# Ten SBUF buffers of split weights: starts at ten different offsets in place of multiples of 2048

## The chip, the cores and the metric

The kernel runs on one core of one Trainium2 chip. The core has TensorE (PE in the profile; its weight loads are listed apart as PEld), VectorE (DVE), ScalarE (ACT), GpSimd (POOL) and SyncE (SP), which here issues all transfers. On-chip memory is SBUF, 128 partitions of which each engine reads and writes the same byte range of all partitions at once, and PSUM, into which matmuls accumulate. The metric is device time in microseconds of one execution; the median of several runs counts.

## What is computed

Two layers on 1024 tokens of width 1024, all in fp32. Layer 0 is attention over a sliding window with sinks, layer 1 a gated linear recurrence (HGRN2); each is followed by an MLP with a squared ReLU, and a norm ends it.

```python
for layer in range(DEPTH):
    h = rmsnorm(x, mix_norm[layer])
    if layer % N_MIXERS == 0:
        y = sliding_window_attention(h, positions, attn_w_qkv[j], attn_b_qkv[j], attn_sinks[j], attn_w_o[j])
    else:
        y = hgrn2_recurrence(h, lbs[layer], hgrn_w_in[j], hgrn_g_norm[j], hgrn_w_o[j])
    x = x + y.astype(x.dtype)
    h = rmsnorm(x, mlp_norm[layer])
    x = x + sqrelu_mlp(h, mlp_w_up[layer], mlp_w_down[layer]).astype(x.dtype)
return rmsnorm(x, final_norm)
```

Nearly all the work is matrix products with weights: QKV and output projections, the four input projections of the recurrence, and 1024 x 4096 up and 4096 x 1024 down in each MLP.

## The kernel before

**Split products.** Weights arrive in fp32. To multiply them in the format fp32r, `weight_split` (line 412) makes two tiles of each 128 x 512 tile: `wh`, the weight rounded to fp32r (a cast on ScalarE or VectorE, whichever the planner finds free), and `wl`, the rest that rounding left (a subtraction on VectorE). Activations are split the same way into pairs of `a` or `t` tiles. `mm3` (line 394) then makes three matmuls of each product: high by high, high by low, low by high. So of three loads of weights two come from a `wh` tile and one from a `wl` tile. In all products but one the split weights are the stationary operand, which LDWEIGHTS puts into TensorE in blocks of 128 columns (512 bytes of each partition), and 512 or 256 columns of activations stream past them. In `qkv` (line 1069) it is the other way: the activations are loaded and 512 columns of `wh` or `wl` stream. In the profile `p<-a,wh` is a matmul that streams an `a` tile, with weights from a `wh` tile, into a PSUM tile of kind p.

The large products follow Strassen's scheme in Winograd's form, which saves products and pays with sums of weight blocks (`m` tiles, on VectorE) and of activations. A weight that is split therefore lies in a `wr` tile (raw, as the transfer brought it), in an `m` tile (a sum of weights) or, in the MLP's down product, in an `a` tile.

**Order.** The program is first recorded as a list of operations with costs in ns (`Schedule.add`). `Schedule.order` (line 185) then plays it through: each engine takes the ready operation of best rank, and each tile gets a slot of its kind, the one that comes free first. `BUFS` (line 41) says how many slots a kind has. The order that this gives is what each engine's queue gets. The costs are constants and functions of the number of columns; no address enters.

**Places in SBUF.** `Buf.handle` (line 111) makes the tile of a slot when it is first used, under a tag such as `wh_3`. All tiles of one tag share one place, as large as the largest of them. Tags are laid one behind the other, each rounded up to 32 bytes. `lay_out` (line 473) runs before all operations are issued and fixes the first places: some constants, then 60 `a`, 18 `t`, 5 `wr`, 5 `wh` and 5 `wl` tiles of 2048 bytes a partition. In the allocation of this kernel the first `a` tile begins at 18432 = 9 x 2048, so all of these lie on multiples of 2048. What comes behind is laid in the order of first use: other constants, the seven `m` buffers and the small `sm` ones. An `m` buffer has 2080 bytes, since attention makes an `m` tile of 128 x 4 x 130 floats (`attend_block`, line 1166, one row group j of 520 bytes for each of four heads). The `m` buffers begin at 209920, 212000 and so on, which is 1024, 1056, 1088, 1120, 1152, 1184 and 1216 past a multiple of 2048.

In attention, ScalarE takes the exponential of each row group of an `m` tile in place (`ACTIVATE m<-m,sm` of 128 x 129), and TensorE transposes each row group (`q<-c,m`: the constant identity streams, the row group is loaded).

Of the kernel before, what the change touches and what calls it, by code (L numbers as in the profile page):

```python
# [2 lines left out]

# [7 lines left out]
F32 = mybir.dt.float32  # L11
# [6 lines left out]
P = 128  # L18
# [4 lines left out]
TH = T // NH  # L23
# [17 lines left out]
BUFS = {"a": 60, "t": 18, "m": 7, "sm": 8, "wr": 5, "wh": 5, "wl": 5, "p": 4, "q": 4}  # L41
CH = 64
LEVELS = 6
HOMES = "aaaaaaaaaaaa"
K_SPANS = ((-1, 3), (2, 6), (5, 8))


class View:
# [34 lines left out]
class Buf:  # L83
# [27 lines left out]
    def handle(self):  # L111
        if self.tile is None:
            tag = f"{self.tag}_{self.slot}"
            self.tile = self.pool.tile(self.shape, self.dtype, tag=tag, name=self.name, bufs=1)
        return self.tile


# [24 lines left out]
class Schedule:  # L142
# [132 lines left out]
    def issue(self, lay_out):  # L275
        ops = self.order()
        lay_out()
        for op in ops:
            op.ways[op.engine][0]()


class Net:
# [190 lines left out]
    def lay_out(self):  # L473

        for v in (self.par, self.ones, self.ident, self.prev_mask, self.mean, self.eps, self.neg, *self.square[:1]):
            v.buf.handle()
        for tag in ("a", "t", "wr", "wh", "wl"):
            for k in range(BUFS[tag]):
                self.pool.tile([P, TH], F32, tag=f"{tag}_{k}", name=f"{tag}_first{k}", bufs=1)

    def spread(self, y, n=TH, r=None):

        r = (r or self.psum("q"))[:, :n]
        for j in range(n // P):
            self.mm(r[:, j * P : j * P + P], y[:, j : j + 1].to_broadcast([P, P]), self.ident, True, True, P, 4)
        return r
# [549 lines left out]
    def k_tiles(self, i):  # L1036
        if self.ks[i] is None:
# [3 lines left out]
            for g, z in enumerate(self.kl[i]):  # L1041
                _, o = self.rows(g)
                self.memset(z[o].bitcast(F32).only("o"), 0.0, "Pool", late)
            if K_SPANS[i][0] < 0:
                for z in self.ks[i] + self.kl[i]:
# [51 lines left out]
    def keys_values(self, n, ps, r):  # L1097
# [14 lines left out]
        for gp in range(2):  # L1112
            self.transpose(pk[:, gp], k[:, gp * P : gp * P + P])
        for i, (first, end) in enumerate(K_SPANS):
            if not first <= n < end:
# [50 lines left out]
    def attend_block(self, g, n, stacks):  # L1166
        i = (n >= 3) + (n >= 6)
        c = slice((n - 1 - K_SPANS[i][0]) * P, (n + 1 - K_SPANS[i][0]) * P)
        tok = slice((n % BPH) * P, (n % BPH) * P + P)
# [485 lines left out]
```

## Time and profile before

| what | value |
|---|---|
| median of 3 runs | 2102.72 us (2101.64 to 2105.72) |
| the profiled execution: its time | 2103.77 us |
| the profiled execution: first to last instruction | 2102.0 us |
| instructions | 35648, of which 12220 matmuls with as many weight loads |
| DMA | 407 MB in the span, 58.5% of the 16 engines' time |

A row of the groups gives the engine and operation, the tiles written and read, the shape and how often; behind the bar the busy time in us and the mean ns of one, then the idle time of the engine ahead of it and what ended that. A row of a tile's view gives the least, median and greatest ns of one. Matmul records overlap: the time that a matmul costs TensorE is the distance between two starts, not its duration. In the chain of work that ended last and in the timeline the first number is the start in us, the second how long the piece lasted, and `x192` says that 192 instructions are merged in it.

### The profile page before, as it was taken

Reading aid. Unit: us, or ns where it says so; the run is one execution under the profiler, and the core shown is the slowest. Engines: PE = TensorE matmul, PEld = TensorE weight load, DVE = VectorE, ACT = ScalarE, POOL = GpSimd, SP = SyncE. Lnnn points to the kernel's source line nnn. Section 1 sums busy time; section 2 is a strip of 40 time slices with the busy share of each in tenths; the row PEclk is TensorE's granted clock in tenths of the full one; section 3 lists DMA queues with packets and bytes.
Section 4 is the critical chain, followed back from the end, with each engine's and each line's share of the span. In section 5 each row is a group of like instructions: output and inputs, shape, how many; then the busy total and the mean of one; then the engine's idle time right before and its main releaser. Section 6 shows DMA issues by size and latency. Waiting matters only on the chain.

```text
span 2102.0 us, 35648 instructions
## 1 busy us (share of the span) xinstructions
PE 2068.4 (98%) x12220; PEld 1738.6 (83%) x12220; DVE 1898.4 (90%) x3922; ACT 1120.0 (53%) x2284; POOL 61.0 (3%) x121
## 2 busy tenths in 40 slices
PE   9999999999999999999999999999999999999998
PEld 7778777888888887888888888888788888888887
DVE  8889899999999989999889888888999999998995
ACT  5567777656565323556444444443755656432453
POOL 4030000000000000000000000000000000000000
PEclk9999999999999999999999999999999999999999
DMA  6212277867778967732322232576787777896742
GB/s 214 79 51 81 86 239 245 297 224 248 231 240 289 313 220 245 236 136 76 101 98 99 96 101 97 202 234 221 270 267 229 244 228 250 284 321 211 238 133 80
DMA packets 225845, 407.43 MB, mean 194 GB/s; under 512 B 25344, under 2 KB 30464, under 8 KB 225664
## 3 DMA queue, kind: packets, MB, share of 16 engines
q1 hardware_dynamic: 225664, 405.16, 58.5%
q8 instruction: 96, 1.57, 0.3%
q14 instruction: 85, 0.70, 0.1%
HBM read 321.17 MB, written 83.89 MB: 193 GB/s over the span
## 4 chain that ended last, share of the span: by engine, by line
PE 38%; DVE 11%; DMA 4%; issue 3%; ACT 1%; POOL 0%; SPq 0%; POOLq 0%; DVEq 0%; ACTq 0%
PE p L336 22%; PE q L336 16%; DVE t L336 4%; DVE a L336 3%; DMA wr<-in_down 2%; DVE wl L336 2%; DVE m L336 2%; ACT t L336 1%; DMA t<-d 1%; DMA wr<-in_up 1%; DMA d<-t 0%; DVE wh L336 0%; DMA wr<-in_win 0%; DMA a<-d 0%; ACT wh L336 0%
## 5 line engine op out<-in xcount | busy, mean ns | idle before, releaser
L336 PE MATMUL p<-a,wh 128*128 128x512 f32 (+1 forms) x2880 | 809.9, 365 | 3.2 <-DVE a L336 2.4
L336 PE MATMUL q<-a,wh 128*128 128x512 f32 x2112 | 654.6, 391 | 7.4 <-ACT t L336 6.1
L336 PEld LDWEIGHTS p<-a,wh 128*128 128x128 f32 x2880 | 514.6, 189 | 89.1 <-DVE a L336 4.0
L336 PE MATMUL p<-a,wl 128*128 128x512 f32 (+1 forms) x1440 | 521.0, 362 | 0.4 <-DVE wl L336 0.4
L336 PEld LDWEIGHTS q<-a,wh 128*128 128x128 f32 x2112 | 389.1, 188 | 85.3 <-ACT t L336 8.4
L336 PE MATMUL q<-a,wl 128*128 128x512 f32 x1056 | 411.1, 390 | 1.7 <-DVE wl L336 1.7
L336 PEld LDWEIGHTS p<-a,wl 128*128 128x128 f32 x1440 | 271.6, 189 | 40.9 <-DVE wl L336 1.3
L336 DVE TENSOR_TENSOR wl<-wr,wh 128x512 fp32r<-128x512 f32 x352 | 240.8, 685 | 6.7 <-ACT wh L336 1.3
L336 DVE TENSOR_TENSOR wl<-m,wh 128x512 fp32r<-128x512 f32 x338 | 230.1, 686 | 10.6 <-ACT wh L336 1.4
L336 PEld LDWEIGHTS q<-a,wl 128*128 128x128 f32 x1056 | 198.3, 188 | 45.6 <-DVE wl L336 3.7
L336 ACT ACTIVATE t<-t 128x512 f32<-128x512 f32 x268 | 168.8, 632 | 122.3 <-DVE t L336 114.9
L336 ACT CAST wh<-wr 128x512 fp32r<-128x512 f32 x249 | 154.0, 619 | 142.8 <-PE p L336 94.7
L336 DVE TENSOR_TENSOR t<-t,t 128x512 f32<-128x512 f32 (+3 forms) x337 | 197.4, 599 | 17.0 <-DMA t<-d 9.9
L336 ACT CAST a<-t 128x512 fp32r<-128x512 f32 (+1 forms) x216 | 130.1, 611 | 148.5 <-PE q L336 78.7
L336 DVE TENSOR_TENSOR a<-t,a 128x512 fp32r<-128x512 f32 (+2 forms) x314 | 205.9, 677 | 2.2 <-ACT a L336 1.7
L336 ACT CAST wh<-m 128x512 fp32r<-128x512 f32 x231 | 143.1, 620 | 113.8 <-PE p L336 47.4
L336 ACT COPY t<-q 128x512 f32<-128x512 f32 (+2 forms) x201 | 112.2, 559 | 104.1 <-PE q L336 87.3
L336 DVE TENSOR_TENSOR m<-wr,wr 128x512 f32<-128x512 f32 (+1 forms) x188 | 120.9, 645 | 17.6 <-DMA wr<-in_down 13.0
L336 PE MATMUL p<-wh,a 128*128 128x512 f32 x384 | 124.9, 396 | 0.7 <-ACT a L336 0.7
L336 DVE TENSOR_TENSOR t<-t,p 128x256 f32<-128x256 f32 x294 | 118.0, 414 | 0.3
L336 PEld LDWEIGHTS q<-t,t 128*64 128x64 f32 (+1 forms) x2160 | 95.4, 144 | 13.6 <-issue 7.6
L336 PE MATMUL q<-t,t 128*64 128x32 f32 (+2 forms) x2160 | 105.3, 229 | 0.0
(129 smaller groups left out, 2392.7 us busy)
## 6 DMA issues: line engine op xcount, KB each, us to landing
t<-d SPq DMA_DIRECT2D x548, 256.0 KB, 4.1
d<-t SPq DMA_DIRECT2D x244, 256.0 KB, 2.7
wr<-in_down SPq DMA_DIRECT2D x224, 256.0 KB, 4.2
wr<-in_up SPq DMA_DIRECT2D x178, 256.0 KB, 3.9
wr<-in_win SPq DMA_DIRECT2D x68, 256.0 KB, 2.9
a<-d SPq DMA_DIRECT2D x60, 256.0 KB, 4.7
wr<-in_wqkv SPq DMA_DIRECT2D x48, 256.0 KB, 2.9
d<-a SPq DMA_DIRECT2D x48, 256.0 KB, 3.9
```

The source lines that it names most:

```text
L336: fn(*[place(a) for a in args], **{k: place(v) for k, v in kw.items()})
```

## The change

The ten buffers `wh_0` to `wh_4` and `wl_0` to `wl_4` are laid alternately, and each gets some unused floats in front, so that its data begin at the listed number of bytes past a multiple of 2048:

| buffer | wh_0 | wl_0 | wh_1 | wl_1 | wh_2 | wl_2 | wh_3 | wl_3 | wh_4 | wl_4 |
|---|---|---|---|---|---|---|---|---|---|---|
| before | 0 | 0 | 0 | 0 | 0 | 0 | 0 | 0 | 0 | 0 |
| after | 4 | 40 | 80 | 96 | 128 | 192 | 256 | 384 | 512 | 768 |
| floats in front | 1 | 2 | 4 | 0 | 8 | 16 | 16 | 32 | 32 | 64 |

`handle` makes the larger tile and hands out a view of it without the floats in front; all else that works on the tile is unchanged. Everything laid behind the ten moves by 768 bytes.

```diff
+W_STARTS = (4, 40, 80, 96, 128, 192, 256, 384, 512, 768)
+SKIP = {}
+_end = 0
+for _k, _start in enumerate(W_STARTS):
+    SKIP[f"{('wh', 'wl')[_k % 2]}_{_k // 2}"] = (_start - _end) // 4
+    _end = -(-_start // 32) * 32
...
             tag = f"{self.tag}_{self.slot}"
-            self.tile = self.pool.tile(self.shape, self.dtype, tag=tag, name=self.name, bufs=1)
+            skip = SKIP.get(tag, 0)
+            if skip:
+                n = math.prod(self.shape[1:])
+                whole = self.pool.tile([self.shape[0], skip + n], self.dtype, tag=tag, name=self.name, bufs=1)
+                self.tile = whole[:, skip:]
+                if len(self.shape) == 3:
+                    self.tile = self.tile.rearrange("p (a b) -> p a b", a=self.shape[1])
+            else:
+                self.tile = self.pool.tile(self.shape, self.dtype, tag=tag, name=self.name, bufs=1)
...
-        for tag in ("a", "t", "wr", "wh", "wl"):
+        for tag in ("a", "t", "wr"):
             for k in range(BUFS[tag]):
                 self.pool.tile([P, TH], F32, tag=f"{tag}_{k}", name=f"{tag}_first{k}", bufs=1)
+        for k in range(BUFS["wh"]):
+            for tag in ("wh", "wl"):
+                name = f"{tag}_{k}"
+                self.pool.tile([P, TH + SKIP[name]], F32, tag=name, name=f"{tag}_first{k}", bufs=1)
```

More of the change, by code (lines that the diff above doesn't have):

```diff
@@ L1 @@
 import heapq
+import math
 from contextlib import ExitStack
```

## The prediction

> **What bounds the kernel now.** I read the page first: the busy shares, the clock the chip granted, then the chain of work that ended last.
>
> ```profile
> span 2102.0 us, 35648 instructions
> PE 2068.4 (98%) x12220; PEld 1738.6 (83%) x12220; DVE 1898.4 (90%) x3922; ACT 1120.0 (53%) x2284; POOL 61.0 (3%) x121
> ...
> PEclk9999999999999999999999999999999999999999
> ...
> PE 38%; DVE 11%; DMA 4%; issue 3%; ACT 1%; POOL 0%; SPq 0%; POOLq 0%; DVEq 0%; ACTq 0%
> PE p L336 22%; PE q L336 16%; DVE t L336 4%; DVE a L336 3%; DMA wr<-in_down 2%; DVE wl L336 2%; DVE m L336 2%; ACT t L336 1%; DMA t<-d 1%; DMA wr<-in_up 1%; DMA d<-t 0%; DVE wh L336 0%; DMA wr<-in_win 0%; DMA a<-d 0%; ACT wh L336 0%
> ```
>
> The matmul stream fills the span and the clock is never held back. The chain names PE for the largest share; the making of split weights (DVE wl, DVE wh, ACT wh) has 2%, 0% and 0% of it. So the first question is what one matmul takes and whether it depends on where its weights lie. The trace's matmul durations overlap, so I take the distance between starts. The chain in order of time has three unbroken stretches at the end, and the timeline of PE has a stretch of 256-column matmuls:
>
> ```profile
> 1965.90 32.71 PE p L336 x143
> 1998.61 43.52 PE q L336 x192
> 2042.13 21.76 PE p L336 x96
> ```
> ```profile
> 400.08 0.40 PE L336 MATMUL p<-t,wh 128*128 128x256 f32 x2
> 400.32 0.28 PE L336 MATMUL p<-t,wl 128*128 128x256 f32 x1
> ...
> 401.40 0.28 PE L336 MATMUL p<-t,wl 128*128 128x256 f32 x1
> 401.52 0.63 PE L336 MATMUL q<-a,wh 128*128 128x512 f32 x2
> ```
>
> 43.52 us over 192 is 226.7 ns for 512 columns; 21.76 over 96 is the same. From 400.08 to 401.52 twelve matmuls start (four rounds of three), 120 ns each for 256 columns. The difference, 106.7 ns for 256 columns, is 0.417 ns a column, and 13.3 ns of each matmul are left over, alike in both sizes. Where that rest comes from the trace doesn't say; the weight load that runs beside each matmul is the nearest candidate. The loads themselves, from the views of the tiles wh and wl (least, median, greatest ns):
>
> ```profile
> L336 PEld LDWEIGHTS p<-a,wh x2880: 186/188/193, 186.3 to 2063.1; 128*128 128x128 f32 x192
> L336 PEld LDWEIGHTS q<-a,wh x2112: 186/188/192, 322.4 to 2041.3; 128*128 128x128 f32 x192
> L336 PEld LDWEIGHTS p<-t,wh x392: 187/192/192, 387.9 to 1776.5; 128*128 128x128 f32 x196
> L336 PE MATMUL p<-wh,a x384: 387/389/504, 5.7 to 186.3; 128*128 128x512 f32 x192
> ```
> ```profile
> L336 PEld LDWEIGHTS p<-a,wl x1440: 186/188/192, 186.7 to 2063.3; 128*128 128x128 f32 x180
> L336 PEld LDWEIGHTS q<-a,wl x1056: 186/188/192, 322.9 to 2041.5; 128*128 128x128 f32 x176
> L336 PEld LDWEIGHTS p<-t,wl x196: 187/192/192, 388.2 to 1776.6; 128*128 128x128 f32 x196
> L336 PE MATMUL p<-wl,a x192: 387/389/477, 6.0 to 186.0; 128*128 128x512 f32 x192
> ```
>
> These six kinds of load come to 2880 + 2112 + 392 + 1440 + 1056 + 196 = 8076; another 384 + 192 = 576 matmuls stream the split weights instead. Two groups of the lines by form give the 256-column part:
>
> ```profile
> L336 PE MATMUL p<-a,wh 128*128 128x256 f32 x784 | 145.5, 283 | 0.3 <-DVE t L336 0.3
> ...
> L336 PE MATMUL p<-a,wl 128*128 128x256 f32 x392 | 110.5, 283 | 0.0
> ```
>
> With the 392 + 196 on t that is 1764 of the 8076; 6312 have 512 columns.
>
> **The change part by part.** It takes no instruction away and adds none: each split buffer becomes a view that begins up to 256 bytes (64 floats) into a slightly larger tile. The planner orders work by costs, none of which knows an address, so order, waits and transfers stay. No DMA writes or reads wh or wl. What can change is the time of an instruction that touches one of the ten, and of those that touch what is laid behind them (m, sm, later constants), which moves by 768 bytes.
>
> *The buffers behind.* In the allocation of the kernel before, the seven m buffers begin at 1024, 1056, 1088 and so on to 1216 past a multiple of 2048. 768 is a multiple of 256, so each keeps its place against every smaller boundary. I cost this at nothing.
>
> *VectorE and ScalarE.* Those m buffers are the trace's own test of uneven starts: three of seven lie 32 bytes past a multiple of 64, while wr lies on multiples of 2048. The same operation with the one and with the other:
>
> ```profile
> L336 DVE TENSOR_TENSOR wl<-wr,wh 128x512 fp32r<-128x512 f32 x352 | 240.8, 685 | 6.7 <-ACT wh L336 1.3 <-PE q L336 0.5 <-DVE wh L336 0.5
> L336 DVE TENSOR_TENSOR wl<-m,wh 128x512 fp32r<-128x512 f32 x338 | 230.1, 686 | 10.6 <-ACT wh L336 1.4
> ...
> L336 ACT CAST wh<-wr 128x512 fp32r<-128x512 f32 x249 | 154.0, 619 | 142.8 <-PE p L336 94.7 <-PE q L336 27.2 <-DMA wr<-in_down 5.5
> ...
> L336 ACT CAST wh<-m 128x512 fp32r<-128x512 f32 x231 | 143.1, 620 | 113.8 <-PE p L336 47.4 <-PE q L336 41.4 <-DVE m L336 24.8
> ...
> L336 DVE CAST wh<-m 128x512 fp32r<-128x512 f32 x107 | 45.6, 426 | 33.6 <-PE p L336 16.7 <-PE q L336 16.6
> ...
> L336 DVE CAST wh<-wr 128x512 fp32r<-128x512 f32 x103 | 43.5, 422 | 26.0 <-PE p L336 20.4 <-DMA wr<-in_wqkv 2.9 <-PE q L336 2.4
> ```
>
> 1 ns, 1 ns and 4 ns apart. Finer starts come from attention, which works on each row group j of an m buffer at 520 j bytes: 0, 8, 16 and 24 past a multiple of 32. In the views of the tiles m and c:
>
> ```profile
> L336 ACT ACTIVATE m<-m,sm x128: 385/391/451, 90.2 to 283.7; 128x129 f32<-128x129 f32 x128
> ...
> L336 PEld LDWEIGHTS q<-c,m x128: 138/141/145, 93.4 to 286.1; 128*128 128x128 f32 x128
> ```
> ```profile
> L336 PEld LDWEIGHTS q<-c,a x80: 137/140/225, 75.8 to 1425.0; 128*128 128x128 f32 x80
> ```
>
> The exponentials, which read and write there, have least and median 6 ns apart, so three starts in four cannot be much dearer than the fourth. I take 1 ns for each of about 1,500 instructions that fill the ten buffers (742 subtractions, 508 + 234 casts): 1.5 us of busy time, hidden behind PE, since their share of the chain is 2% for wl and 0% for wh. With that cover gone it costs 1.5 us. A start at 4 bytes, off a multiple of 8, is wh_0's alone and no row shows it in a long run. From above: its casts on VectorE lose their rate and take a subtraction's 685 in place of some 424 ns, 261 ns on a fifth of 234, 12 us, and half of that reaches the path where VectorE, busy 90%, has no slack. From below, nothing; the 32-byte rows give no reason for a gain. I take nothing, as the m rows are nearest.
>
> *Weight loads.* For LDWEIGHTS the start matters to 8076 instructions, so one nanosecond on all is 8 us. Loads from m at 8, 16 and 24 take 138 to 145 ns against 137 and a median of 140 from tile a on multiples of 2048: 1 ns. These are plain fp32 loads; the split ones are fp32r and take 188. What covers a slower load is seen in the timeline:
>
> ```profile
> 2010.01 0.62 PE L336 MATMUL q<-a,wh 128*128 128x512 f32 x2
> 2010.01 0.19 PEld L336 LDWEIGHTS q<-a,wh 128*128 128x128 f32 x1
> 2010.24 0.19 PEld L336 LDWEIGHTS q<-a,wl 128*128 128x128 f32 x1
> ```
>
> A load starts with the matmul before its own and ends after 188 of 226.7 ns: 39 ns of cover. The 256-column matmuls start each 120 ns with loads of 192, so loads also overlap each other. A load longer by 1 to 4 ns (188 to 192 is the whole spread in the rows) costs nothing. If instead it took its nanosecond from the stream, on the four buffers off a multiple of 64 (4, 40, 80, 96; two fifths, 3230 loads), that is 3.2 us. I take 0.5 us in all, and 3 us as its upper end.
>
> *Streaming.* The 576 matmuls that stream wh or wl have a median of 389, as have those that stream a. An uneven start could add one step to a run of 512; 1 ns each is 0.6 us. I take nothing.
>
> Sum: 2102.0 us of span, 1.8 us around it (this execution took 2103.8), plus 0.5. That execution lay 1.1 us above the median of the runs, 2102.7; so 2102.7 + 0.5, some **2103 us**. Its own range, from the 3.2 + 1.5 us above and the spread of the runs (2101.6 to 2105.7), is 2100 to 2108.
>
> A rule of the Trainium skill speaks against the change: "SBUF — State Buffer", section "Specifications (TRN2)", gives lines of 16 bytes and says that each crossing to a new line pays. A load of 512 bytes a partition touches 32 such lines from an even start and 33 from 4 or 40. If the 13.3 ns were those 32 lines, an estimate by that page, a 33rd would add 0.4 ns to a fifth of the loads, 0.7 us; no row here shows it.
>
> **Rivals.** *Slower: fp32r loads out of wh_0 and wl_0 hold up the stream.* A load runs beside a matmul, and each matmul has 13.3 ns that streaming doesn't explain, which could be the load's reads taking turns with it. If a start off 16 bytes (4 and 40) splits each read in two, the 13.3 double for a fifth of 8076 loads: 1615 x 13.3 = 21.5 us, 2124. If 64 is the boundary, two fifths, 43 us, 2146. For it: PE has no slack, and no row has fp32r with an uneven start. Against: the fp32 loads from m. It decides once those matmuls stand over 229.3 ns apart (4.2 us over 1615).
>
> *Faster: loads and streams collide because all lie on multiples of 512.* If staggering freed the 13.3 ns on every load, PE would save 107 us; VectorE becomes the bound long before:
>
> ```profile
> 390.00:700.00 310.00, 309.92 (x1759) 272.60 (x1758) 286.88 (x578) 176.74 (x299) 0.00 (x0) 1.00 0.77 253
> ```
>
> There (windows: PE, PEld, DVE, ACT) VectorE is busy 286.88 of 310 us, 7% idle that it partly needs for waits. I allow half, 53 us: 2049. Against: the load reads a short block while the stream runs through all addresses, so a collision for good is unlikely, and the rest is the same 13.3 in 256-column and 512-column matmuls on different tiles.
>
> *The change does more than it says:* a view cut from a larger tile could bring other waits. If the share of wl on the chain, 2% or 42 us, grew by half, 2124.
>
> **How the numbers follow.** What a measurement of this kernel can tell from no change is about 0.2%, 4.2 us. No effect 0.52, of which 0.48 lie within 4.2 us, 0.03 above and 0.01 below; loads slower 0.33; other waits 0.04; collisions freed 0.11. So slower 0.40, same 0.48, faster 0.12. The range runs from 2098 to 2130: it takes in the 21.5 us of the slower rivals and the casts' 6 us, and leaves out the 43 us end (some 0.08) and the gain (some 0.11).
>
> **What would show it.** Right: 35648 instructions, the loads' median still 188, the stretches at the end of the chain still 226.7 ns a matmul, the casts 619 and 424, subtractions 685. Wrong, towards slower: a longer distance between starts in stretches that use one buffer, periodic with it; casts in DVE's rows with a second value near 685. Wrong, towards faster: a distance under 226 ns. Other waits: more instructions, and wl or wh with more than 2% of the chain.

## The result, and the profile after

The changed kernel takes 2114.08 us (median of 4 runs, 2113.8 to 2116.98) against 2103.52 us before: a ratio of 1.0053, 95% interval 1.0036 to 1.0070. It is slower by 10.6 us.

From the page of the changed kernel: the span, the busy shares, the chain's shares by engine and by line, and two groups of matmuls (behind the bar busy us and mean ns, then the idle time ahead of them):

```profile
span 2112.5 us, 35648 instructions
...
PE 2089.0 (99%) x12220; PEld 1738.4 (82%) x12220; DVE 1900.8 (90%) x3922; ACT 1121.5 (53%) x2284; POOL 60.8 (3%) x121
...
PE 82%; DVE 9%; ACT 3%; DMA 3%; issue 3%; SPq 0%; POOL 0%; POOLq 0%; ACTq 0%; DVEq 0%
...
L351 PE MATMUL p<-a,wh 128*128 128x512 f32 (+1 forms) x2880 | 815.9, 367 | 0.4 <-ACT t L351 0.3
L351 PE MATMUL q<-a,wh 128*128 128x512 f32 x2112 | 660.9, 394 | 1.5 <-ACT t L351 1.0
```

The instructions are the same in number. VectorE, ScalarE and the weight loads are as busy as before; PE has 20.6 us more (2089.0 against 2068.4). Only half of that reaches the end: PE's idle time shrank from 33.6 us (2102.0 less 2068.4) to 23.5. The two groups show where. On the page of the kernel before they read:

```profile
L336 PE MATMUL p<-a,wh 128*128 128x512 f32 (+1 forms) x2880 | 809.9, 365 | 3.2 <-DVE a L336 2.4
L336 PE MATMUL q<-a,wh 128*128 128x512 f32 x2112 | 654.6, 391 | 7.4 <-ACT t L336 6.1
```

Matmuls that had waited 3.2 and 7.4 us, most of it for a DVE or ACT result, now wait 0.4 and 1.5. A slower PE gives the others time to get ahead, and PE's share of the chain goes from 38% to 82%.

The loads, matmuls and casts themselves, from the view of tile wh (least, median, greatest ns), two rows of the kernel before and then the changed kernel:

```profile
L336 PE MATMUL q<-a,wh x2112: 387/389/504, 322.7 to 2041.5; 128*128 128x512 f32 x192
...
L336 ACT CAST wh<-wr x249: 602/621/655, 7.4 to 2017.8; 128x512 fp32r<-128x512 f32 x125
```

```profile
L351 PEld LDWEIGHTS p<-a,wh x2880: 185/188/193, 189.0 to 2074.0; 128*128 128x128 f32 x192
...
L351 PEld LDWEIGHTS q<-a,wh x2112: 186/188/193, 325.9 to 2051.8; 128*128 128x128 f32 x192
L351 PE MATMUL q<-a,wh x2112: 387/393/504, 326.1 to 2052.0; 128*128 128x512 f32 x192
...
L351 ACT CAST wh<-wr x249: 602/621/656, 7.8 to 2025.8; 128x512 fp32r<-128x512 f32 x125
L351 ACT CAST wh<-m x231: 602/621/690, 328.1 to 1935.8; 128x512 fp32r<-128x512 f32 x116
```

No load and no cast is longer: their medians are still 188 and 621 ns. The records of these matmuls grew by 4 ns in the median, from 389 to 393; as matmul records overlap, what this costs is read from the distance between starts. The last long stretches of the chain of waits in the changed kernel:

```profile
1963.78 44.45 PE p L351 x192
2008.22 44.44 PE q L351 x192
2052.66 22.20 PE p L351 x96
```

44.44 us over 192 matmuls is 231.5 ns; before, the same 192 took 43.52 us, 226.7 ns. Counted over the starts in the trace, 512-column matmuls between others of their kind that load split weights stand 231.5 ns apart (5768 of them), and stood 227.6 (5754). Before, 83% of these distances were the trace's 226 or 227; after, 15%, and nearly all the others scatter from 224 to 241. The 256-column ones came closer together, 118.6 in place of 120.0 ns.

Grouped by the buffer that the next load reads (the profile leaves buffer numbers out; the order of the program's matmuls gives them), the changed kernel's 512-column distances are:

| buffer | wh_0 | wl_0 | wh_1 | wl_1 | wh_2 | wl_2 | wh_3 | wl_3 | wh_4 | wl_4 |
|---|---|---|---|---|---|---|---|---|---|---|
| start | 4 | 40 | 80 | 96 | 128 | 192 | 256 | 384 | 512 | 768 |
| ns | 232.8 | 231.9 | 232.0 | 231.8 | 233.0 | 231.0 | 232.0 | 231.8 | 229.1 | 227.9 |

A start at 128, which is even by every small measure, costs as much as one at 4. That speaks against a price for uneven starts, and the experiments start there.

### The profile page after: what moved, and what is told of

It reads as the page before. It is cut to its first block, busy times and chain, and to the rows that moved or that the text cites. A ratio compares the mean times of both kernels' runs of the same rounds, so it can differ in the third digit from the quotient of the medians.

```text
span 2112.5 us, 35648 instructions
## 1 busy us (share of the span) xinstructions
PE 2089.0 (99%) x12220; PEld 1738.4 (82%) x12220; DVE 1900.8 (90%) x3922; ACT 1121.5 (53%) x2284; POOL 60.8 (3%) x121
## 4 chain that ended last, share of the span: by engine, by line
PE 82%; DVE 9%; ACT 3%; DMA 3%; issue 3%; SPq 0%; POOL 0%; POOLq 0%; ACTq 0%; DVEq 0%
PE p L351 43%; PE q L351 39%; DVE t L351 4%; DVE a L351 2%; ACT t L351 2%; DVE wl L351 1%; DVE m L351 1%; DMA wr<-in_up 1%; ACT a L351 1%; DMA a<-d 1%; DMA a<-in_x 1%; DMA d<-t 0%; DMA t<-d 0%; ACT m L351 0%; ACT wh L351 0%
## 5 line engine op out<-in xcount | busy, mean ns | idle before, releaser
L351 PE MATMUL q<-a,wl 128*128 128x512 f32 x1056 | 415.4, 394 | 1.1 <-DVE wl L351 1.1
```

The source lines that it names most:

```text
L351: fn(*[place(a) for a in args], **{k: place(v) for k, v in kw.items()})
```

## The experiments

The theories: **phase**, that the distance depends on where the load's addresses stand to those of the stream that runs beside it; **fine starts**, that only starts off 16 or 64 bytes cost; **mixture**, that changes from load to load cost; **boundary**, that a load crossing a multiple of 512 costs, whatever the stream does.

**u64: all ten at one start, 64.**

```diff
         for tag in ("a", "t", "wr", "wh", "wl"):
+            if tag == "wh":
+                self.pool.tile([P, 64 // 4], F32, tag="pad", name="pad", bufs=1)
```

> All ten split buffers begin 64 bytes past a multiple of 2048; the streamed a and t tiles stay on multiples. Theory phase (what counts is where a load's addresses stand to those of the stream beside it): each 512-column matmul stands some 231 to 232 ns from the next, as with the changed kernel, or at another steady value, and the time is 2108 to 2116 us. Rival fine starts (only starts off 16 or 64 bytes cost): 226.7 ns and 2103 us, as before. Rival mixture (only the difference from one load to the next costs): 226.7 ns, 2103 us. Rival boundary (a load that crosses a multiple of 512 costs, wherever the stream is): 231 to 232 ns, 2114 us.

Measured: 2119.14 us, ratio 1.0068 (1.0043 to 1.0094), outside the 2116 that I had allowed. The chain of waits and two rows of the timeline of PE, where twelve 256-column matmuls start:

```profile
2013.07 44.80 PE q L336 x192
```
```profile
400.67 0.39 PE L336 MATMUL p<-t,wh 128*128 128x256 f32 x2
...
402.03 0.62 PE L336 MATMUL q<-a,wh 128*128 128x512 f32 x2
```

44.80 over 192 is 233.3 ns, and in this stretch of the trace it is an even 233, 233, 234, with no scatter. These 256-column matmuls have 1.36 us for twelve, 113.3 ns in place of 120; the mean over all distances of 256-column matmuls is 115.6 in place of 120.0. So mixture isn't needed for a loss: one start for all makes a longer distance, 233.3 against 231.5. And a start on 64 isn't safe, which fine starts had said it was.

**u256: all ten at 256** (the same edit with 256).

> All ten begin 256 bytes past a multiple of 2048. Phase: another relation of load and stream than before, so 227 to 232 ns (in the changed kernel the buffer at 768, which is 256 past a multiple of 512, stood at 228, the one at 256 at 232), 2103 to 2114 us, and not the same as at 64. Fine starts and mixture: 226.7 ns, 2103 us. Boundary: 231 to 232 ns, 2114 us.

Measured: 2102.01 us, 0.9991 (0.9979 to 1.0004): no change. Boundary falls here, since each of these loads crosses a multiple of 512; phase had left open whether 256 would cost. In the chain the 192 take what they took before, within 0.05 us:

```profile
1997.08 43.57 PE q L336 x192
```

**all64: the streamed tiles move along** (the pad stands ahead of tag "a").

> The streamed tiles a and t, the raw wr and the ten split buffers all begin 64 bytes past a multiple of 2048, so loads stand to streams as before. Phase, fine starts and mixture: 226.7 ns, 2103 us, no change. Boundary: 231 to 232 ns, 2114 us.

Measured: 2104.64 us, 1.0001 (0.9990 to 1.0012). Its chain:

```profile
1998.14 43.68 PE q L336 x192
```

Loads at 64 cost nothing when the streams lie at 64 too, and 1.0068 when the streams stay at 0 (u64): what counts is the difference of load and stream.

**fine: the four fine starts alone.**

```diff
-W_STARTS = (4, 40, 80, 96, 128, 192, 256, 384, 512, 768)
+W_STARTS = (4, 40, 80, 96, 512, 512, 512, 512, 512, 512)
```

> Only wh_0, wl_0, wh_1 and wl_1 keep their starts (4, 40, 80, 96); the other six begin at 512 past a multiple of 2048. Fine starts: the whole loss of the change stays, 2114 us, all of it on these four buffers. Phase: four loads in ten stand badly, so some 40% of the loss in the distances (loads from the four at 232, from the six at 227 ns) and 2106 to 2110 us. Mixture: much as phase. Boundary: as phase.

Measured: 2115.04 us, 1.0047 (1.0031 to 1.0064). By the time alone this is what fine starts says, and more than phase allowed. The distances say otherwise: ahead of a load from the four they are 231.4 to 232.6 ns, and ahead of a load from the six, all on multiples of 512, 229.8 and not 227. A load that stands badly also disturbs those behind it: directly behind a load from the four, the distance ahead of one from the six is 232.4 ns, and only behind some nine loads from the six is it back at 227.

**coarse: the other six alone.**

```diff
-W_STARTS = (4, 40, 80, 96, 128, 192, 256, 384, 512, 768)
+W_STARTS = (0, 0, 0, 0, 128, 192, 256, 384, 512, 768)
```

> The four fine starts are gone (wh_0, wl_0, wh_1, wl_1 on multiples of 2048); 128, 192, 256, 384, 512 and 768 stay for the other six. Phase: loads at 128, 192 and 384 (three of ten) disturb, those at 256, 512 and 768 not: mean distance 228.5 to 231 ns, 2106 to 2113 us. Fine starts: 226.7 ns, 2103 us.

Measured: 2109.10 us, 1.0027 (1.0018 to 1.0037). Without a fine start half of the loss is there; mean distance 229.7 ns. Ahead of a second load from the buffer at 128 it is 236.0, ahead of one from 384 it is 232.3, ahead of one from 192 it is 231.1, between loads at 0 it is 227.8. The losses of the two parts, 1.0047 and 1.0027, don't add up to that of the whole, 1.0053.

**phase: the curve.** A kernel of matmuls alone; the core of it:

```python
N_EACH = 16
...
def series(load, stream, n):
    ps = net.psum("pq"[len(got) % 2])
    for k in range(N_EACH):
        net.mm(ps[:, :n], loads[:, load // 4 : load // 4 + P], streams[:, stream // 4 : stream // 4 + n], k == 0, k == N_EACH - 1, n)
...
for load in range(0, 512, 4):
    series(load, 0, TH)
for load in range(0, 256, 8):
    series(load, 0, TH // 2)
for stream in (4, 16, 64, 128):
    for load in range(0, 256, 32):
        series(load, stream, TH)
```

> None of the network is computed: TensorE alone makes series of 16 matmuls in fp32r, each with a load of 128 columns (512 bytes a partition) from one tile and a stream from another, both tiles on multiples of 2048. In series after series the load begins 0, 4, 8 ... 508 bytes into its tile with 512 columns streamed from 0; then 0, 8 ... 248 with 256 columns; then 0, 32 ... 224 with 512 columns streamed from 4, 16, 64 and 128. Theory phase: the distance of two starts is a curve over load start minus stream start that repeats every 256 bytes (226.7 ns at 0 and 256, 233.3 at 64, as the kernel showed), and moves with the stream's start; with 256 columns 120 ns at 0 and 114 at 64. Rival alignment: starts off 16 or 64 bytes cost more than their neighbours on 64, and the stream's start moves nothing.

The chain of waits has one row for each series of 16. These are the series with loads at 4, 64, 120, 128, 228 and 256, then 320 and 376, streams at 0; at the end streams at 4 with a load at 0, at 64 with a load at 64, and at 128 with a load at 64 and one at 128:

```profile
12.59 3.72 PE q L336 x16
...
68.41 3.72 PE p L336 x16
...
120.52 3.65 PE p L336 x16
...
127.87 3.74 PE p L336 x16
...
220.71 3.63 PE q L336 x16
...
246.48 3.66 PE p L336 x16
...
305.95 3.72 PE p L336 x16
...
358.06 3.65 PE p L336 x16
...
544.41 3.79 PE p L336 x16
...
611.85 3.63 PE p L336 x16
...
641.59 3.68 PE p L336 x16
...
649.00 3.64 PE p L336 x16
```

3.63 us over 16 is 226.9 ns, 3.74 is 233.8. The kernel ran once, in 667.09 us; what follows is read from the trace of that run. VectorE is busy for 1.0 us of it, so the curve doesn't come from VectorE's reads and writes.

**The curve with streams at 0.** Taking the last eleven distances of a series, when it has settled, the starts 120, 144, 156, 204, 228, 252 and 256 stand at 226.6 to 226.7; nothing is lower; the others lie between 227.8 and 236.6. (The first series, at 0, is left out: its matmuls began up to 427 ns apart, while the granted clock was 0.68 on the average, from 7.00 to 12.40 us.) The curve from 256 to 508 repeats the one from 0 to 252: 233.1 at 64 and at 320, 226.6 at 120 and 226.7 at 376, 233.7 at 128 and at 384; no pair is more than 0.2 ns apart.

**Other streams.** With streams at 64 or 128 the curve moves along: load 64 on stream 64 and load 128 on stream 128 have 226.6, load 64 on stream 128 has 229.2, as load 192 on stream 0; all 16 of these series lie within 1.1 ns of the curve. So phase holds for streams on 0, 64 and 128, with a period of 256 bytes, and alignment doesn't order the curve: 228, off 8 bytes, is on the floor and 128 is not.

Two things phase had not said. A stream that begins at 4 has 233.4 to 240 ns with every load tried, though by the difference alone the loads at 0 and 160 would be on the floor, and one at 16 has 230.8 to 236.5, for seven of the eight loads more than their difference alone gives: a stream's own start has a price. And with 256 columns the load at 64 has 117.7 here and not 114, so the gain seen in u64 is not a property of the one start.

**u128, wh120, wh228, wh4: the curve put back into the kernel.** u128 is the edit of u64 with 128. The other three give the five wh the start named, past multiples of 256, and put the five wl on multiples of 256:

```diff
-W_STARTS = (4, 40, 80, 96, 128, 192, 256, 384, 512, 768)
+W_STARTS = (120, 256, 376, 512, 632, 768, 888, 1024, 1144, 1280)
...
+W_STARTS = (228, 256, 484, 512, 740, 768, 996, 1024, 1252, 1280)
...
+W_STARTS = (4, 256, 260, 512, 516, 768, 772, 1024, 1028, 1280)
```

> All ten begin 128 bytes past a multiple of 2048. Theory phase, from the series (233.7 ns at 128): 512-column matmuls some 233 ns apart, 2115 to 2121 us as with 64. Rival boundary at 256 alone would say the same; rival fine starts (16 or 64 bytes): 226.7 ns, 2103 us.

> The five wh begin 120 bytes past a multiple of 256, off any multiple of 16, the five wl on multiples of 256. Phase, from the series (226.6 ns at 120 once settled, 226.7 at 0): most distances at 226 to 227 ns and 2102 to 2108 us, if loads that change between the two starts settle within a matmul or two; if they don't settle, a mean of 229 to 232 ns and 2108 to 2114 us. Fine starts: all 5384 wh loads dear, more than in the changed kernel, 2115 us or more.

> The five wh begin 228 bytes past a multiple of 256, off any multiple of 8; the five wl on multiples of 256. Phase, from the series (226.7 ns at 228 and at 0): 226.7 ns between matmuls that load split weights, as with 120; where wh streams, a stream off 64 bytes costs some 4 ns on 576 matmuls, 2 us; 2102 to 2108 us. A cost of the start's own alignment (4 bytes): 2115 us or more.

> The five wh begin 4 bytes past a multiple of 256, the five wl on multiples of 256. Phase, from the series (232.5 ns at 4): wh loads, two of three, stand badly and disturb the third, 230 to 233 ns, 2110 to 2120 us. A cost of alignment: the same here, but then the same with 228 as well.

Measured: u128 2121.08 us, 1.0083 (1.0068 to 1.0098); wh120 2104.95 us, 1.0005 (0.9993 to 1.0017); wh228 2109.26 us, 1.0026 (1.0013 to 1.0038); wh4 2118.03 us, 1.0062 (1.0043 to 1.0081). The same stretch of the chain in u128, in wh120, in wh228 and in wh4:

```profile
2016.44 44.61 PE q L336 x192
```
```profile
2000.07 43.52 PE q L351 x192
```
```profile
2004.50 44.37 PE q L351 x192
```
```profile
2012.40 44.37 PE q L351 x192
```

The best-aligned start of the four, 128, is dear, and 120, off 16 bytes, costs nothing: 43.52 us, to the digit the value before. wh4 came as phase had said, with a mean distance of 231.4 ns. wh228 is a miss. Alone, 228 stands at 226.7, but in turn with wl at 0 it doesn't settle: distances of 224 and of 229 to 236 follow each other, mean 230.6. With 120 and 0 in turn they do settle, at a mean of 227.2. So the curve of single starts isn't enough for a mixture, and mixture was right in so far. A cost of the start's own alignment isn't what wh228 shows either: that was to be 2115 us or more, and as much as in wh4. In the QKV products, where wh and wl stream, all of these starts cost: the mean distance there is 228.5 ns before, 232.5 in wh120, 231.9 in wh228 and 236.6 in wh4.

**t192: only the t tiles moved, to beat both.** All ten back on a multiple of 256, with a and wr; only the t tiles, whose fp32r streams beside split weights all have 256 columns, begin 192 past one:

```diff
         for tag in ("a", "t", "wr", "wh", "wl"):
+            if tag in ("t", "wr"):
+                self.pool.tile([P, {"t": 192, "wr": 64}[tag] // 4], F32, tag=f"pad_{tag}", name=f"pad_{tag}", bufs=1)
```

> A version that could beat both: a, wr, wh and wl stay on multiples of 256, the 18 t tiles begin 192 past one. Of the streams from t, 588 are 256-column matmuls with split weights; to them the loads then stand at 64, where the kernel with all ten at 64 had 113 to 114 ns in place of 120. Phase: these 588 gain some 6 ns each, 3.7 us, the 512-column ones (which stream a) stay at 226.7; 2099 to 2102 us. If the gain doesn't reach the end: 2103 us. Rivals fine starts and boundary: no change.

Measured: 2099.92 us against 2103.15, 0.9984 (0.9974 to 0.9994), faster than before, if barely, and than the changed kernel. The timeline of PE where such a series begins:

```profile
398.72 0.40 PE L336 MATMUL p<-t,wh 128*128 128x256 f32 x2
398.96 0.28 PE L336 MATMUL p<-t,wl 128*128 128x256 f32 x1
399.08 0.39 PE L336 MATMUL p<-t,wh 128*128 128x256 f32 x2
...
399.76 0.39 PE L336 MATMUL p<-t,wh 128*128 128x256 f32 x2
```

The first three take 0.36 us, 120 ns each, the next six 0.68, 113.3 each: it settles after a few. Over the matmuls on t between others of 256 columns the mean is 116.2 ns against 119.8, some 2 us for 588 of them; the end moved by 3.2, and the interval holds both.

## Why the prediction was right and wrong

**What bounds the kernel** was right: PE's start-to-start distance is the one thing that the change moved, and it moved the time. The reading that each matmul has 13.3 ns beyond its columns, and that the load beside it is the likely owner, holds as far as the loads' starts move that part: 13.3 became 18.1 on the average (231.5 less 213.4).

**VectorE and ScalarE, and the buffers behind**: right. ScalarE's casts keep the median of 621 ns that the rows of wh show, VectorE's casts have medians of 420 to 426 ns (420 and 421 before), and VectorE's busy time went from 1898.4 to 1900.8 us.

**The step that failed is "Weight loads"**, and with it the forecast of no change: "A load longer by 1 to 4 ns ... costs nothing. If instead it took its nanosecond from the stream, on the four buffers off a multiple of 64 ..., that is 3.2 us." I asked whether a load would get longer and found 39 ns of cover. The loads did not get longer, 188 ns as before, and the cover was untouched; the stream beside them did, by some 4 ns in 227. The rows that I took as the test, the plain fp32 loads from m at 8, 16 and 24, give a load's duration, which is the number that stays the same. And the buffers at fault were not only the four off 64, though these alone can make as much as the whole change (1.0047 in fine): in coarse the ones at 128, 192 and 384, which I had costed at nothing, make half of the loss, and in u128 all ten make 18 us.

That the range of 2098 to 2130 us holds the 2114 is in good part luck. The forecast in its middle, 2103, was no change, and the part of the range above 2108 stood there for the slower rivals and for casts that lose their rate, none of which came as described.

**The slower rival** had the right place and the wrong condition. The time did go into the stream beside a load, though that their reads take turns is not shown; but the rival had a start off 16 or 64 bytes as the condition and a doubled 13.3 ns as the price. The condition, for streams on 0, 64 and 128, is the difference of load and stream modulo 256; the price at most starts is 4 to 7 ns a matmul. Its 21.5 us lies near PE's own loss of 20.6, by a share and a price that were both wrong, and twice as high as the measured 10.6, for a term that I left out: PE's waits shrink as its matmuls grow. Busy time against span gives 20.6 and 10.5 us more for the change, 26.3 and 16.4 for u64, 30.2 and 19.5 for u128: some 10 us are swallowed in each of the three.

**The faster rival** fell. In the series no start gets under 226.6 ns: for 512 columns no staggering tried here frees any of the 13.3 ns, and the kernel with all on multiples of 512 already stood on that floor. Only the 256-column matmuls had something to free (120 to 113.3).

**Other waits**: not seen; there are 35648 instructions as before, and in the changed kernel wl has 1% of the chain and wh 0%. Of the signs that I named, the longer distance came, but only in part "periodic" with the buffer, since a badly standing load disturbs those behind it: even ahead of loads from 256 the mean is 232.0.

The rule of the Trainium skill that I weighed ("SBUF — State Buffer", section "Specifications (TRN2)": each crossing to a new line of 16 bytes pays) doesn't show in these runs as a price of the load's start: 120, which touches a 33rd line, stands at 226.6 ns as 256 does, without the 0.4 ns of my estimate, and 128, which doesn't, at 233.7.

What stays open is what in the chip repeats every 256 bytes. That loads and streams get in each other's way by address is shown by all64 and the series; which part of the chip does it no run here shows. Why 120 and 0 in turn settle, and 228 and 0 don't, is open too.

## What to carry to other kernels

Lay the stationary and the streamed operands of long fp32r products on starts with the same remainder modulo 256, and the streams on multiples of 64 (0, 64 and 128 were tried); that, and not the alignment of the load's start, kept 512-column matmuls at their floor here. When PE is the bound, read the distance between starts, not the durations of loads: the distance grew by 1.7%, from 227.6 to 231.5 ns, while the loads kept 188 ns and the median of the matmuls' own records moved from 389 to 393. Part of a slower PE is paid out of its own waits, here 10 of 20 us, so look at what they are before pricing a loss in full.

## What the runs showed of the hardware

I had not expected the place of the weights to set the distance of the matmuls so evenly: 192 of them took 43.52 us with loads and streams on multiples of 512, 44.80 with the loads at 64, and 44.61 with the loads at 128; the stretch of 192 before it took 44.80 and 44.62 in these two kernels. Nor that one relation can be bad for 512 columns (233.3 for 226.7 ns) and good for 256 (113.3 for 120 where it settled).
